# The softmax divisors of an attention: from four small products, a copy and four transposes to one product with repeated ones

## The chip, the cores and the metric

The kernel runs on one core of a Trainium2 chip. A core has engines that each run their own list of instructions in order: TensorE (PE; its weight loads are a row of their own, PEld), VectorE (DVE), ScalarE (ACT), GpSimd (POOL) and SyncE (SP, which issues most of the transfers). TensorE writes its products into eight banks of a small memory (PSUM); VectorE and ScalarE read them from there. The metric is the device time of one execution in microseconds (us).

## What is computed

Two layers of a backbone over 1024 latent tokens with 256 context tokens. Each layer projects the tokens, runs two groups of heads, joins their outputs by one product, and ends in an MLP. One group is an attention with 8 heads of 64 value channels, the other a recurrence (RWKV-7) over the tokens in both directions. The change touches the attention:

```python
def attend(q, k, v):
    s = jnp.einsum('bqhd,bkhd->bhqk', q, k).astype(jnp.float32) * MLA_SCALE
    p = jax.nn.softmax(s, axis=-1).astype(v.dtype)
    return jnp.einsum('bhqk,bkhd->bqhd', p, v)
```

Latent queries see all 1280 keys, context queries the 256 context keys. The kernel forms the exponentials first, multiplies them with the values, and divides at the end by the sum of the exponentials of each query. The change is in how this divisor gets to where it is needed.

## The kernel before, in words

Before and after the two head groups the layers are projections, norms and an MLP, whose products run on TensorE in three passes each (high and low halves). Between them lies one stage per layer, built by `heads`: attention and recurrence together, in one list of work. The profile has these stages at about 510 to 1130 us (layer 0) and 2590 to 3185 us (layer 1).

The attention goes through the heads, and in each head through tiles of queries: two tiles of 512 latent queries, and in layer 0 one of 256 context queries. So there are 16 + 16 tiles of 512 and 8 of 256, 40 in all. In a tile:

- SP loads the queries (`Qraw`), ACT and POOL split them (`Qh`, `Ql`).
- For the maximum of each row, TensorE makes a rough product of queries and keys (L723) and VectorE reduces it (L725, L726), one 128 rows by up to 512 keys at a time.
- For every 128 keys TensorE makes the scores (L750, keys in rows, queries in columns), ACT takes the exponential (`P`, L755), POOL adds it into the kept sums `Ps` (L759), and every second one TensorE multiplies with the values (L744) into `ps_o`, as two halves in rows 0 to 63 and 64 to 127.
- ACT copies one half out (`oa`, L767), VectorE adds the other (`ob`, L768). Now `ob` has 64 channels in rows and the queries in columns.
- The kept sums `Ps` still have 128 rows. `total` (L772) adds them up: per 128 queries a product with `Ps` as weights and one column of ones going past, so that the sums come to lie in rows, one column per 128 queries. VectorE takes the reciprocal of these 4 (or 2) columns (`rc`, L775), POOL repeats each number 64 times along its row (`rx`, L776), TensorE transposes that (`turned`, L780), and VectorE multiplies `ob` by the result (L783). Then `ob` goes to memory by a transfer.

The recurrence goes through 10 steps of 128 tokens in each direction. In a step VectorE masks the products of the tokens (`A`, L391), solves triangular systems by 31 pairs of small instructions that each wait for the one before (`mult` and `total`, L444 and L448), and adds to the states (`S`, L550, L551) and outputs (`ys`, `yo`, L570, L634); TensorE has many small products in between (L387, L401, L411, L481, L493, L527 to L560, L610).

All work in a stage is a list of units. Each has an engine, a duration that its author has written beside it (in ns), what it reads and writes, and for a product that lands in PSUM a kind of bank: six banks `g` serve all of both groups, one bank `o` the values. `Units.run` plays the list through with these durations. At each step it takes, among the units that could start within `slack` ns of the earliest, the one with the longest remaining path, plus a number from `RANKS_HEADS` for its name. The order in which units are taken is the order of the instructions on each engine, for good. It also gives each product a bank: the one of its kind that comes free first by the durations written. On the chip an engine then goes through its instructions in that order, and waits by semaphores where an operand is late or a bank still being read.

Of the kernel before, what the change touches and what calls it, by code (L numbers as in the profile page):

```python
# [12 lines left out]
ALU = mybir.AluOpType  # L13
# [86 lines left out]
def sp_ns(n, k=1):  # L100
# [3 lines left out]


RANKS_IN = {"scaled": 14500, "kf": 1500, "squares k": 4000, "spread c": 19500}
RANKS_HEADS = ({"halves": 6003, "total": -414, "A": 21222, "m1p": -12501, "m1": -28360, "y": -24249, "f2": 3549, "values": -12745, "BKt": -21292,
                "end3": -17483, "yp": -1704, "begin1": -12967, "put": -46488, "f1a": -16985, "f3a": -17647, "f1": -1812, "rows": 2463,
                "sums": -3935, "max": 16985, "mult": -21876, "scores": 798},
               {"begin1": -12967, "f2": -5416, "rows": -1699, "sums": 2772, "max": 16985, "put": -49846, "f3a": -11034, "mult": -34975,  # L110
                "f1a": -36576, "total": 5499, "f1": -2926, "A": 16339, "BKt": -29802, "values": -13309, "y": -24249, "m1": -19796, "yp": -2244,
                "m1p": -12501, "end3": -17483, "scores": 6271, "halves": 19842})
RANKS_OUT = {"copied": -19500, "squares": 28500, "vectors": 14000, "scaled": -7500, "low": -1500, "weights": -7500, "product": -10000, "stage": -3500}


# [150 lines left out]
class Trunk:  # L266
# [36 lines left out]
    def heads(self, li, ard, bvd, pc, gated, ysd, kd, vd, qd, qrd, krr, catd):  # L303

        with ExitStack() as es:
            e1 = self.pool(es, "hd", 1)
            ps = self.pool(es, "hps", 1, space=PSUM)
            banks = {k: [ps.tile([128, 512], F32, name=f"ps_{k}{j}") for j in range(n)] for k, n in (("g", 6), ("o", 1))}
            tiles = {"Y": [ps.tile([128, 32, 16], F32, name=f"ps_Y{li}")]}


            for name, n, shape in (("YF", 1, [128, 32, 32]), ("AX", 1, [128, 32, 32]), ("XM", 1, [128, 32, 32]), ("Y0", 1, [128, 32, 16]), ("tmp", 1, [128, 144]),
# [4 lines left out]
                                   ("Ql", 3, [97, 512]), ("identr", 1, [128, 128]), ("Kh", 2, [97, NT]), ("Kl", 2, [97, NT]), ("Qraw", 1, [96, 512]), ("Kraw", 1, [96, NT])):  # L317
                tiles[name] = [e1.tile(shape, F32R if name in ("Kh", "Kl", "Qh", "Ql", "nm", "identr") else F32, name=f"{name}{li}{j}") for j in range(n)]
            us = Units(59, RANKS_HEADS[li], dict(PE=110, ACT=20, DVE=115, Pool=80, SP=2300), False, True, 0.745, 0.395, 80)
            self.recurrence(us, tiles, li, ard, bvd, pc, gated, ysd, catd)  # L320
            us.group = 1
            self.attention(us, tiles, li, kd, vd, qd, qrd, krr, catd)
            with self.tc.manual_schedule(engines=ENGINES):
                us.run(banks)
# [337 lines left out]
    def attention(self, us, tiles, li, kd, vd, qd, qrd, krr, catd):  # L662


        nc = self.nc
        last = li == L - 1
        qtt = LAT if last else LAT + ALL[:1]
        Kh, Kl, V, Qraw, Qh, Ql, P, Ps, o2, nm, nm3 = (tiles[k] for k in ("Kh", "Kl", "V", "Qraw", "Qh", "Ql", "P", "Ps", "ob", "nm", "nm3"))
        Kraw, o1, rx, rc, identr = (tiles[k][0] for k in ("Kraw", "oa", "rx", "rc", "identr"))
        NK, NQ, NP, NO = len(Kh), len(Qh), len(P), len(o2)  # L670
        c1 = self.c("unit")[:, 1:2]

# [10 lines left out]
        for j in range(NK):  # L683
            us("ACT", act_ns(NT), [], lambda j=j: nc.scalar.copy(Kh[j][64:96], Kraw[64:96]), r=[("Kraw", "rope")], w=[("Kh", j, "rope")])
            us("Pool", pool_ns(NT), [], lambda j=j: nc.gpsimd.tensor_tensor(Kl[j][64:96], Kraw[64:96], Kh[j][64:96].bitcast(F32), op=ALU.subtract),
               r=[("Kraw", "rope"), ("Kh", j, "rope")], w=[("Kl", j, "rope")])
# [18 lines left out]
        def tile(h, p, q, kh, kl, khk, klk, v, vk, e, t0, tl):  # L705
            t, nq = slice(t0, t0 + tl), tl // 128
            nkt = 10 if t0 >= TC else 2
            jr, jq = us.turn("Qraw", len(Qraw)), us.turn("Q", NQ)
            raw, qh, ql, m1, m3 = Qraw[jr], Qh[jq], Ql[jq], nm[jq], nm3[jq]
# [11 lines left out]
            for i in range(nq):  # L721
                for n, (k0, kn) in enumerate(ktt):
                    x = us("PE:max", 140 + kn * 0.28, [], lambda b, i=i, k0=k0, kn=kn: nc.tensor.matmul(b[:, :kn], qh[0:96, 128 * i:128 * i + 128], kh[0:96, k0:k0 + kn], start=True, stop=True), 220,  # L723
                           bank="g", r=[("Qh", jq)] + khk, rows=91)
                    us("DVE", 63 + kn * 1.048, [], lambda b, i=i, n=n, kn=kn: nc.vector.tensor_reduce(m3[:, i, n:n + 1], b[:, :kn], AXIS_X, ALU.max), w=[("nm3", jq, i, n)], free=x)  # L725
            us("DVE", 72, [], lambda: nc.vector.tensor_reduce(m1[:, :nq], m3[:, :nq, :len(ktt)], AXIS_X, ALU.max, negate=True),  # L726
               r=[("nm3", jq, i, n) for i in range(nq) for n in range(len(ktt))], w=[("nm", jq)])
# [5 lines left out]
            x = us("PE:rows", 55 + 111 * nq, [], rows, 200, bank="g", r=[("nm", jq), "identr"], rows=64)  # L733
# [3 lines left out]
            js = us.turn("Ps", 2)  # L737
            sums = Ps[js][:, :tl]
# [8 lines left out]
            for n in range(nkt):  # L747
# [6 lines left out]
                x = us("PE:scores", 60 + tl * 1.344, [], pe, 155, bank="g", r=khk + klk + [("Qh", jq), ("Qh", jq, "row"), ("Ql", jq), ("Ql", jq, "row")], rows=90)  # L754
# [5 lines left out]
                if n % 2:  # L760
                    kw = dict(use=out) if out else dict(bank="o")
                    x = us("PE:values", 84 + 1.805 * tl, [], pair(n - 1, [P[i][:, :tl] for i in jp[-2:]]), r=[("P", i) for i in jp[-2:]] + [vk, ("O", h, t0)], w=[("O", h, t0)], rows=119, **kw)
                    out = out or x

            jo = us.turn("ob", NO)
            o = o2[jo][:, :tl]
            x1 = us("ACT", 180 + tl * 0.835, [], lambda b: nc.scalar.copy(o1[:, :tl], b[64:128, :tl]), r=[("O", h, t0)], w=["oa"], use=out)  # L767
            us("DVE:halves", 75 + tl * 1.04, [], lambda b: nc.vector.tensor_tensor(o, b[0:64, :tl], o1[:, :tl], op=ALU.add), r=["oa", ("O", h, t0)], w=[("ob", jo)], free=out)  # L768

            def total(b):  # L770
                for i in range(nq):
                    nc.tensor.matmul(b[:, i:i + 1], Ps[js][:, 128 * i:128 * i + 128], c1, start=True, stop=True)  # L772

            x = us("PE", 845 / 4 * nq, [], total, 145, bank="g", r=[("Ps", js, 128 * i) for i in range(nq)], rows=1)
            us("DVE", 92, [], lambda b: nc.vector.reciprocal(rc[:, :nq], b[:, :nq]), w=["rc"], free=x)  # L775
            us("Pool", 206 + 54 * nq, [], lambda: nc.gpsimd.tensor_copy(rx[:, :nq], rc[:, :nq].unsqueeze(2).to_broadcast([128, nq, 64])), r=["rc"], w=["rx"])  # L776

            def turned(b):
                for i in range(nq):
                    nc.tensor.transpose(b[0:64, 128 * i:128 * i + 128], rx[:, i], self.ident)  # L780

            x = us("PE", 96 * nq, [], turned, 280, bank="g", r=["rx"], rows=121)
            us("DVE", 75 + tl * 1.04, [], lambda b: nc.vector.tensor_tensor(o, o, b[0:64, :tl], op=ALU.mult), w=[("ob", jo)], free=x)  # L783
            if h < 7:
                us("SP", sp_ns(tl / 2), [], lambda: nc.sync.dma_start(catd[0][q, p, t], o), r=[("ob", jo)])
            else:
# [953 lines left out]
```

## Time and profile before

| | before |
|---|---|
| median of 3 runs | 3976.65 us (3976.02 to 3977.47) |
| profiled execution: its time | 3976.51 us |
| profiled execution: span of the trace | 3974.7 us |
| PE busy | 3819.7 us (96%) |
| DVE busy | 2463.1 us (62%) |
| ACT busy | 1826.9 us (46%) |
| POOL busy | 1267.8 us (32%) |
| mean granted TensorE clock | 0.969 of full speed |

The profile is of one execution. Its instructions carry the line of the kernel and the names of the tiles; a fp32 product shows as two matmuls. Busy times are sums over an engine's own row. An instruction's record holds its start-up too, so records of one engine overlap by some 60 to 90 ns; what an instruction costs its engine in a full queue is read from its start to the start of the next.

### The profile page before, as it was taken

How to read it: one execution, taken by the hardware profiler on the slowest of the kernel's cores; microseconds unless marked ns; L12 is line 12 of the kernel's file. 1: busy time of each engine (PE TensorE's matmuls, PEld its weight loads, DVE VectorE, ACT ScalarE, POOL GpSimd, SP SyncE). 2: the span in 40 equal slices, each digit the busy share in tenths (PEclk: the TensorE clock that was granted, in tenths of full speed). 3: DMA queues.
4: the chain of work that ended last, by engine and by line, in shares of the span. 5: the costliest groups of instructions: out<-in, count | busy, mean ns of one | idle time of the engine just before them, and what ended most of it. 6: DMA issues, size and time to landing. Idle time of an engine off the chain costs nothing.

```text
span 3974.7 us, 66881 instructions
## 1 busy us (share of the span) xinstructions
PE 3819.7 (96%) x26144; PEld 2939.4 (74%) x26144; DVE 2463.1 (62%) x4563; ACT 1826.9 (46%) x3125; POOL 1267.8 (32%) x1850
## 2 busy tenths in 40 slices
PE   5999989999999999999998999999999999999998
PEld 2766766777778888888887766666777688777787
DVE  4476377777537455555337377577778465767666
ACT  4355467777635112222114355567777644333332
POOL 1244174455621000000001244365445704334320
PEclk9999989999999999999999999989899999999999
DMA  6256633332252122222113144532232351111111
GB/s 217 67 172 200 202 117 95 99 102 85 70 171 85 59 80 86 79 70 80 38 43 132 44 153 155 199 112 64 87 106 76 98 189 32 54 43 48 54 48 59
DMA packets 279708, 394.22 MB, mean 99 GB/s; under 512 B 60512, under 2 KB 192576, under 8 KB 279392
## 3 DMA queue, kind: packets, MB, share of 16 engines
q1 hardware_dynamic: 278992, 389.36, 30.7%
q8 instruction: 206, 3.38, 0.4%
q14 instruction: 110, 0.90, 0.1%
q10 hardware_dynamic: 400, 0.59, 0.1%
HBM read 288.45 MB, written 101.42 MB: 98 GB/s over the span
## 4 chain that ended last, share of the span: by engine, by line
PE 76%; DVE 9%; DMA 3%; issue 2%; ACT 2%; POOL 1%; SPq 0%; DVEq 0%; POOLq 0%; ACTq 0%
PE qm L938 41%; PE pm_m L938 8%; PE ps_g L750 5%; PE ps_o L744 3%; PE ps_g L723 2%; PE ps_g L387 2%; PE qm L951 1%; PE ps_g L536 1%; PE ps_g L527 1%; PE ps_g L546 1%; PE ps_g L481 1%; PE ps_g L401 1%; PE ps_g L557 1%; PE ps_g L560 1%; PE pm_n L1192 1%
## 5 line engine op out<-in xcount | busy, mean ns | idle before, releaser
L938 PE MATMUL qm<-hh,wh 128*128 128x512 f32 (+1 forms) x1488 | 556.3, 374 | 6.9 <-DVE x L1536 6.9
L938 PE MATMUL qm<-hh,wl 128*128 128x512 f32 (+1 forms) x1488 | 554.7, 373 | 0.7 <-DVE wl L976 0.7
L938 PE MATMUL qm<-hl,wh 128*128 128x512 f32 (+1 forms) x1488 | 555.0, 373 | 0.0
L759 POOL TENSOR_TENSOR Ps<-Ps,P 128x128 f32<-128x128 f32 x1024 | 433.8, 462 | 308.2 <-ACT P L755 307.9
L975 ACT CAST wh<-wr 128x1024 fp32r<-128x1024 f32 x149 | 155.8, 1045 | 445.6 <-PE qm L938 399.9
L938 PE MATMUL pm_m<-hh,wh 128*128 128x512 f32 (+4 forms) x896 | 339.1, 378 | 3.7 <-ACT o L1251 3.1
L938 PE MATMUL pm_m<-hl,wh 128*128 128x512 f32 (+4 forms) x896 | 330.0, 368 | 1.3 <-POOL hl L925 1.3
L938 PE MATMUL pm_m<-hh,wl 128*128 128x512 f32 (+4 forms) x896 | 330.3, 369 | 0.2 <-DVE wl L976 0.2
L938 PEld LDWEIGHTS qm<-hh,wh 128*128 128x128 f32 x1488 | 279.6, 188 | 64.7 <-DVE x L1536 9.0
L938 PEld LDWEIGHTS qm<-hh,wl 128*128 128x128 f32 x1488 | 280.2, 188 | 55.0 <-DVE wl L976 1.4
L938 PEld LDWEIGHTS qm<-hl,wh 128*128 128x128 f32 x1488 | 279.6, 188 | 55.2 <-DVE hl L1432 1.2
L1536 DVE SCALAR_TENSOR_TENSOR x<-qm,mods,x 128x512 f32<-128x512 f32 x280 | 196.3, 742 | 174.4 <-PE qm L938 174.1
L938 PE MATMUL qm<-uh,wl 128*128 128x512 f32 (+1 forms) x768 | 274.0, 357 | 2.1 <-DVE wl L976 2.1
L938 PE MATMUL qm<-uh,wh 128*128 128x512 f32 (+1 forms) x768 | 275.1, 358 | 0.0
L938 PE MATMUL qm<-ul,wh 128*128 128x512 f32 (+1 forms) x768 | 273.8, 356 | 0.0
L976 DVE TENSOR_TENSOR wl<-wr,wh 128x1024 fp32r<-128x1024 f32 x149 | 187.7, 1260 | 131.1 <-ACT wh L975 130.9
L1459 DVE SCALAR_TENSOR_TENSOR x<-qm,mods,x 128x512 f32<-128x512 f32 x160 | 119.7, 749 | 196.3 <-PE qm L938 192.8
L725 DVE TENSOR_REDUCE nm<-ps_g 128x1 f32<-128x512 f32 (+1 forms) x400 | 213.4, 583 | 38.1 <-PE ps_g L723 36.9
L938 PEld LDWEIGHTS pm_m<-hh,wh 128*128 128x128 f32 (+2 forms) x896 | 169.4, 189 | 68.4 <-issue 31.2
L755 ACT ACTIVATE P<-ps_g 128x512 f32<-128x512 f32 (+1 forms) x336 | 188.6, 586 | 64.9 <-PE ps_g L750 50.4
L938 PEld LDWEIGHTS pm_m<-hl,wh 128*128 128x128 f32 (+2 forms) x896 | 169.3, 189 | 33.6 <-POOL hl L925 2.2
L938 PEld LDWEIGHTS pm_m<-hh,wl 128*128 128x128 f32 (+2 forms) x896 | 169.6, 189 | 30.7 <-issue 0.7
(358 smaller groups left out, 8591.7 us busy)
## 6 DMA issues: line engine op xcount, KB each, us to landing
wr<-in_w SPq DMA_DIRECT2D x90, 512.0 KB, 3.6
BV<-bv SPq DMA_DIRECT2D x40, 768.0 KB, 4.9
raw<-in_ada_w SPq DMA_DIRECT2D x48, 512.0 KB, 3.9
AR<-ar SPq DMA_DIRECT2D x40, 512.0 KB, 7.3
wr<-in_w_in SPq DMA_DIRECT2D x37, 512.0 KB, 3.8
aw<-in_ada_w SPq DMA_DIRECT2D x32, 512.0 KB, 4.2
bv<-bk SPq DMA_DIRECT2D x32, 512.0 KB, 3.0
ar<-ar SPq DMA_DIRECT2D x32, 512.0 KB, 3.6
```

Source lines behind the costliest of these rows:

```text
L387: nc.tensor.matmul(b[:, 128 * j:128 * j + 128], BK[d][half(e), c, p], AR[d][half(e), 2 * p + c], start=True, stop=True)
L723: x = us("PE:max", 140 + kn * 0.28, [], lambda b, i=i, k0=k0, kn=kn: nc.tensor.matmul(b[:, :kn], qh[0:96, 128 * i:128 * i + 128], kh[0:96, ...
L725: us("DVE", 63 + kn * 1.048, [], lambda b, i=i, n=n, kn=kn: nc.vector.tensor_reduce(m3[:, i, n:n + 1], b[:, :kn], AXIS_X, ALU.max), w=[("n ...
L744: nc.tensor.matmul(b[64 * r:64 * r + 64, :tl], v[:, n + r, q], ps[r], start=n == 0, stop=n + 2 == nkt)
L750: nc.tensor.matmul(b[:, :tl], x[:, 128 * n:128 * n + 128], y[:, :tl], start=i == 0, stop=i == 2)
L755: us("ACT", 195 + tl * 0.835, [], lambda b, j=j: nc.scalar.activation(P[j][:, :tl], b[:, :tl], AF.Exp, scale=SCALE), w=[("P", j)], free=x)
L759: us("Pool:sums" if n == 1 else "Pool", 415, [], lambda a=a, b=P[j][:, c:c + 128], c=c: nc.gpsimd.tensor_tensor(sums[:, c:c + 128], a, b, ...
L938: self.nc.tensor.matmul(out, a, b, start=n == 0, stop=n == last)
L975: us("ACT", 947, [], lambda: nc.scalar.copy(wh, raw), r=[key], w=[("wh", j)])
L976: us("DVE:weights", 1135, [], lambda: nc.vector.tensor_tensor(wl, raw, wh.bitcast(F32), op=ALU.subtract), r=[key, ("wh", j)], w=[("wl", j)])
L1459: us("DVE", dve_ns(tl), [u[1]], lambda b: nc.vector.scalar_tensor_tensor(X(m, a), b[:, :tl], self.mods[li][:, 8 * gate + m, s:s + 1], X(m, ...
L1536: z = us("DVE", dve_ns(512), [z], lambda b, m=m, a=a, f=f: nc.vector.scalar_tensor_tensor(X(m, a), b, f, X(m, a), ALU.mult, ALU.add), r=[" ...
```

## The change

One product takes the place of `total` and `turned`: the weights are the column of ones, repeated 64 times, and the kept sums `Ps` go past, 512 (256) columns. Its 64 rows are all the same, the sum of each query's exponentials, in the layout of `ob`. VectorE takes the reciprocal of this whole 64x512 block (into `oa`, which the addition of the halves has by then read) and multiplies `ob` by it. The column `rc`, its repetition `rx` on POOL and the transposes go. The ranks are set anew, the product has a rank of its own name, and `slack`, 59 before, is 67 in layer 0 and 93 in layer 1.

```diff
--- before.py
+++ after.py
@@ -104,12 +104,12 @@
 
 
 RANKS_IN = {"scaled": 14500, "kf": 1500, "squares k": 4000, "spread c": 19500}
-RANKS_HEADS = ({"halves": 6003, "total": -414, "A": 21222, "m1p": -12501, "m1": -28360, "y": -24249, "f2": 3549, "values": -12745, "BKt": -21292,
-                "end3": -17483, "yp": -1704, "begin1": -12967, "put": -46488, "f1a": -16985, "f3a": -17647, "f1": -1812, "rows": 2463,
-                "sums": -3935, "max": 16985, "mult": -21876, "scores": 798},
-               {"begin1": -12967, "f2": -5416, "rows": -1699, "sums": 2772, "max": 16985, "put": -49846, "f3a": -11034, "mult": -34975,
-                "f1a": -36576, "total": 5499, "f1": -2926, "A": 16339, "BKt": -29802, "values": -13309, "y": -24249, "m1": -19796, "yp": -2244,
-                "m1p": -12501, "end3": -17483, "scores": 6271, "halves": 19842})
+RANKS_HEADS = ({"A": 15017, "values": -14650, "BKt": -37124, "y": -8577, "max": 16985, "put": -55711, "m1p": -10723, "sums": 6443,
+                "scores": 10819, "f1": -2328, "total": 1188, "halves": 11193, "f3a": -14590, "end3": 5410, "f2": 3549, "rows": 2774,
+                "begin1": -12967, "m1": -28327, "yp": -349, "mult": -46018, "f1a": -36247, "slack": 67},
+               {"m1": -19227, "yp": -2244, "y": -34405, "mult": -22669, "values": -13309, "BKt": -29802, "rows": 13653, "f1a": -55013, "A": 24283,
+                "f1": -1805, "put": -36636, "f2": 26845, "f3a": -11034, "scores": 6271, "halves": 19842, "m1p": -12501, "end3": -17483,
+                "sums": 1538, "max": 12049, "begin1": -19234, "total": 7372, "slack": 93})
 RANKS_OUT = {"copied": -19500, "squares": 28500, "vectors": 14000, "scaled": -7500, "low": -1500, "weights": -7500, "product": -10000, "stage": -3500}
 
 
@@ -312,11 +312,11 @@
             for name, n, shape in (("YF", 1, [128, 32, 32]), ("AX", 1, [128, 32, 32]), ("XM", 1, [128, 32, 32]), ("Y0", 1, [128, 32, 16]), ("tmp", 1, [128, 144]),
                                    ("Z", 2, [128, 4, 2, 64]), ("BV", 2, [128, 1536]), ("AR", 4, [128, 8, 128]), ("G", 2, [128, 32, 64]), ("XT", 1, [128, 32, 64]),
                                    ("S", 4, [128, 4, 64]), ("ys", 2, [128, 4, 128]), ("gt", 2, [128, 512]), ("sq", 1, [128, 512]), ("rs8", 1, [128, 8]), ("P", 6, [128, 512]),
-                                   ("Ps", 2, [128, 512]), ("oa", 1, [64, 512]), ("ob", 2, [64, 512]), ("rx", 1, [128, 4, 64]), ("rc", 1, [128, 4]), ("nm", 3, [128, 4]),
+                                   ("Ps", 2, [128, 512]), ("oa", 1, [64, 512]), ("ob", 2, [64, 512]), ("nm", 3, [128, 4]),
                                    ("nm3", 3, [128, 4, 3]), ("A", 2, [128, 32, 2, 64]), ("BKt", 1, [128, 32, 64]), ("V", 2, [128, 10, 128]), ("Qh", 3, [97, 512]),
                                    ("Ql", 3, [97, 512]), ("identr", 1, [128, 128]), ("Kh", 2, [97, NT]), ("Kl", 2, [97, NT]), ("Qraw", 1, [96, 512]), ("Kraw", 1, [96, NT])):
                 tiles[name] = [e1.tile(shape, F32R if name in ("Kh", "Kl", "Qh", "Ql", "nm", "identr") else F32, name=f"{name}{li}{j}") for j in range(n)]
-            us = Units(59, RANKS_HEADS[li], dict(PE=110, ACT=20, DVE=115, Pool=80, SP=2300), False, True, 0.745, 0.395, 80)
+            us = Units(RANKS_HEADS[li]["slack"], RANKS_HEADS[li], dict(PE=110, ACT=20, DVE=115, Pool=80, SP=2300), False, True, 0.745, 0.395, 80)
             self.recurrence(us, tiles, li, ard, bvd, pc, gated, ysd, catd)
             us.group = 1
             self.attention(us, tiles, li, kd, vd, qd, qrd, krr, catd)
@@ -666,7 +666,7 @@
         last = li == L - 1
         qtt = LAT if last else LAT + ALL[:1]
         Kh, Kl, V, Qraw, Qh, Ql, P, Ps, o2, nm, nm3 = (tiles[k] for k in ("Kh", "Kl", "V", "Qraw", "Qh", "Ql", "P", "Ps", "ob", "nm", "nm3"))
-        Kraw, o1, rx, rc, identr = (tiles[k][0] for k in ("Kraw", "oa", "rx", "rc", "identr"))
+        Kraw, o1, identr = (tiles[k][0] for k in ("Kraw", "oa", "identr"))
         NK, NQ, NP, NO = len(Kh), len(Qh), len(P), len(o2)
         c1 = self.c("unit")[:, 1:2]
 
@@ -767,20 +767,10 @@
             x1 = us("ACT", 180 + tl * 0.835, [], lambda b: nc.scalar.copy(o1[:, :tl], b[64:128, :tl]), r=[("O", h, t0)], w=["oa"], use=out)
             us("DVE:halves", 75 + tl * 1.04, [], lambda b: nc.vector.tensor_tensor(o, b[0:64, :tl], o1[:, :tl], op=ALU.add), r=["oa", ("O", h, t0)], w=[("ob", jo)], free=out)
 
-            def total(b):
-                for i in range(nq):
-                    nc.tensor.matmul(b[:, i:i + 1], Ps[js][:, 128 * i:128 * i + 128], c1, start=True, stop=True)
-
-            x = us("PE", 845 / 4 * nq, [], total, 145, bank="g", r=[("Ps", js, 128 * i) for i in range(nq)], rows=1)
-            us("DVE", 92, [], lambda b: nc.vector.reciprocal(rc[:, :nq], b[:, :nq]), w=["rc"], free=x)
-            us("Pool", 206 + 54 * nq, [], lambda: nc.gpsimd.tensor_copy(rx[:, :nq], rc[:, :nq].unsqueeze(2).to_broadcast([128, nq, 64])), r=["rc"], w=["rx"])
-
-            def turned(b):
-                for i in range(nq):
-                    nc.tensor.transpose(b[0:64, 128 * i:128 * i + 128], rx[:, i], self.ident)
-
-            x = us("PE", 96 * nq, [], turned, 280, bank="g", r=["rx"], rows=121)
-            us("DVE", 75 + tl * 1.04, [], lambda b: nc.vector.tensor_tensor(o, o, b[0:64, :tl], op=ALU.mult), w=[("ob", jo)], free=x)
+
+            x = us("PE:total", 45 + 1.79 * tl, [], lambda b: nc.tensor.matmul(b[0:64, :tl], c1.to_broadcast([128, 64]), sums, start=True, stop=True), 160, bank="g", r=[("Ps", js, c) for c in range(0, tl, 128)], rows=121)
+            us("DVE", 75 + tl * 1.04, [], lambda b: nc.vector.reciprocal(o1[:, :tl], b[0:64, :tl]), w=["oa"], free=x)
+            us("DVE", 75 + tl * 1.04, [], lambda: nc.vector.tensor_tensor(o, o, o1[:, :tl], op=ALU.mult), r=["oa"], w=[("ob", jo)])
             if h < 7:
                 us("SP", sp_ns(tl / 2), [], lambda: nc.sync.dma_start(catd[0][q, p, t], o), r=[("ob", jo)])
             else:
```

The new ranks and the new lengths move instructions all through both stages. Two places show what matters for the divisors. In the tables below `ps_g_3470` to `ps_g_3475` are the six banks `g` of layer 0, a row is a line of the kernel, an operation, what it writes and reads, its columns, and in brackets what it waits for. In the kernel after, L771 is the new product, L772 the reciprocal of 64x512 and L773 the multiplication; lines up to L768 are the same in both.

On TensorE, at the second tile of layer 0, before: the sums go into bank 3471, the transposes of another tile's divisors into 3470, and bank 3471 is written again after those, a pair of values (L744), a group of scores (L750) and two row maxima (L723).

```order
L772 MATMUL ps_g_3471<-ct,Ps_3511 128x1 [waits Activation_49,Pool_49]
L772 MATMUL ps_g_3471<-ct,Ps_3511 128x1 [waits Pool_49] x3
L780 MATMUL ps_g_3470<-ct,rx_3515 64x128 [waits Activation_49,Pool_49]
L780 MATMUL ps_g_3470<-ct,rx_3515 64x128 x3
L744 MATMUL ps_o_3476<-P_3504,V_3526 64x512
L744 MATMUL ps_o_3476<-P_3505,V_3526 64x512
L750 MATMUL ps_g_3475<-Qh_3528,Kh_3536 128x512 [waits Activation_49]
L750 MATMUL ps_g_3475<-Qh_3528,Kl_3538 128x512
L750 MATMUL ps_g_3475<-Ql_3531,Kh_3536 128x512
L723 MATMUL ps_g_3474<-Kh_3536,Qh_3529 128x512 [waits Activation_49]
L723 MATMUL ps_g_3470<-Kh_3536,Qh_3529 128x512 [waits DVE_49]
L723 MATMUL ps_g_3471<-Kh_3536,Qh_3529 128x512 [waits DVE_49]
```

The same tile after: the sums go into bank 3473, three products for row maxima follow, and then comes one of the recurrence (L493) into bank 3473 again.

```order
L771 MATMUL ps_g_3473<-Ps_3511,ct 64x512 [waits Activation_49,Pool_49]
L723 MATMUL ps_g_3474<-Kh_3534,Qh_3527 128x512 [waits Activation_49]
L723 MATMUL ps_g_3475<-Kh_3534,Qh_3527 128x512
L723 MATMUL ps_g_3470<-Kh_3534,Qh_3527 128x512
L493 MATMUL ps_g_3473<-XT_3493,XM_3480 32x32 [waits DVE_49,Activation_49]
L493 MATMUL ps_g_3473<-XT_3493,XM_3480 32x32 [waits Activation_49]
L493 MATMUL ps_g_3473<-XT_3493,XM_3480 32x32 x14
L723 MATMUL ps_g_3471<-Kh_3534,Qh_3527 128x512
```

So the transposes are gone, and the bank of the sums, which VectorE frees by its reciprocal, is now wanted again after three products.

On VectorE, around the second tile's reciprocal, before: the multiplication of one tile, the reciprocal of 4 columns, and then work of the recurrence (L444, L448), row maxima (L725) and the next tile's halves (L768).

```order
L783 TENSOR_TENSOR ob_3513<-ob_3513,ps_g_3470 64x512 [waits PE_49]
L775 RECIPROCAL rc_3516<-ps_g_3471 128x4 [waits Pool_49]
L444 TENSOR_TENSOR tmp_3482<-AX_3479,ps_Y_3477 128x31 [waits Activation_49]
L725 TENSOR_REDUCE nm_3521<-ps_g_3474 128x1 [waits PE_49]
L768 TENSOR_TENSOR ob_3514<-ps_o_3476,oa_3512 64x512 [waits Activation_49]
L448 TENSOR_TENSOR ps_Y_3477<-ps_Y_3477,tmp_3482 128x31 [waits DVE_49]
L725 TENSOR_REDUCE nm_3521<-ps_g_3470 128x1 [waits PE_49]
L725 TENSOR_REDUCE nm_3521<-ps_g_3471 128x1 [waits PE_49]
```

The same reciprocal after: it has 512 columns, the multiplication (L773) follows one instruction later, and behind these stand the row maxima of four banks.

```order
L772 RECIPROCAL oa_3512<-ps_g_3473 64x512 [waits PE_49]
L444 TENSOR_TENSOR tmp_3482<-AX_3479,ps_Y_3477 128x100 [waits DVE_49]
L773 TENSOR_TENSOR ob_3514<-ob_3514,oa_3512 64x512 [waits DVE_49]
L448 TENSOR_TENSOR ps_Y_3477<-ps_Y_3477,tmp_3482 128x25x4 [waits DVE_49]
L725 TENSOR_REDUCE nm_3519<-ps_g_3474 128x1 [waits PE_49]
L725 TENSOR_REDUCE nm_3519<-ps_g_3475 128x1 [waits PE_49]
L725 TENSOR_REDUCE nm_3519<-ps_g_3470 128x1 [waits PE_49]
L725 TENSOR_REDUCE nm_3519<-ps_g_3471 128x1 [waits PE_49,Activation_49]
```

The multiplication, which stood ahead of or far behind its reciprocal, now follows it at once, and the row maxima stand right behind both.

## Rows read from the trace of the kernel before

**Rows 1.** The page: TensorE's busy time; the chain that ended last, by engine.

```profile
PE 3819.7 (96%) x26144; PEld 2939.4 (74%) x26144; DVE 2463.1 (62%) x4563; ACT 1826.9 (46%) x3125; POOL 1267.8 (32%) x1850
...
PE 76%; DVE 9%; DMA 3%; issue 2%; ACT 2%; POOL 1%; SPq 0%; DVEq 0%; POOLq 0%; ACTq 0%
```

**Rows 2.** Busy times by stretch, both stages: stretch, length, busy time per engine, clock, DMA.

```profile
500.00:1131.00 631.00, 603.22 (x6898) 434.31 (x6899) 440.55 (x1158) 440.00 (x792) 364.88 (x694) 0.94 0.32 94
2565.00:3190.00 625.00, 591.51 (x6518) 429.32 (x6517) 436.46 (x1120) 431.74 (x762) 344.63 (x659) 0.92 0.32 97
```

**Rows 3.** DVE's groups by shape, 512 to 1130: busy us, mean ns | idle before.

```profile
L768 DVE TENSOR_TENSOR ob<-ps_o,oa 64x512 f32<-64x512 f32 x16 | 10.8, 677 | 9.0 <-ACT oa L767 8.7
...
L768 DVE TENSOR_TENSOR ob<-ps_o,oa 64x256 f32<-64x256 f32 x8 | 3.3, 412 | 6.8 <-ACT oa L767 6.8
...
L775 DVE RECIPROCAL rc<-ps_g 128x4 f32<-128x4 f32 x16 | 2.8, 176 | 11.1 <-PE ps_g L772 11.1
L621 DVE TENSOR_SCALAR rs<-ps_g 128x8 f32<-128x8 f32 x10 | 1.7, 166 | 13.8 <-PE ps_g L618 13.7
L775 DVE RECIPROCAL rc<-ps_g 128x2 f32<-128x2 f32 x8 | 1.3, 166 | 5.2 <-ACT P L755 3.7 <-PE ps_g L772 1.4
```

**Rows 4.** DVE in order of time, two reciprocals: start us, length us, instruction.

```profile
1055.62 0.15 DVE L775 RECIPROCAL rc<-ps_g 128x2 f32<-128x2 f32 x1
1055.70 0.66 DVE L634 TENSOR_TENSOR yo<-ps_g,yo 128x512 f32<-128x512 f32 x1
...
3005.48 0.17 DVE L775 RECIPROCAL rc<-ps_g 128x4 f32<-128x4 f32 x1
3005.57 3.05 DVE L725 TENSOR_REDUCE nm<-ps_g 128x1 f32<-128x512 f32 x5
```

**Rows 5.** PE in order of time: sums, transposes, a 128x512 fp32 product.

```profile
893.60 0.95 PE L772 MATMUL ps_g<-ct,Ps 128*128 128x1 f32 x8
894.48 3.37 PE L387 MATMUL ps_g<-AR,BV 64*128 64x128 f32 x40
897.78 0.63 PE L780 MATMUL ps_g<-ct,rx 128*64 128x128 f32 x4
898.16 0.37 PE L750 MATMUL ps_g<-Qh,Kh 97*128 97x256 f32 x1
...
990.61 1.02 PE L610 MATMUL ps_g<-ys,ct 128*128 128x512 f32 x2
991.57 1.08 PE L744 MATMUL ps_o<-P,V 128*64 128x512 f32 x4
```

**Rows 6.** PE in order of time, behind the sums at 3003.96.

```profile
3004.88 1.47 PE L723 MATMUL ps_g<-Kh,Qh 96*128 96x512 f32 x4
3006.28 1.08 PE L744 MATMUL ps_o<-P,V 128*64 128x512 f32 x4
3007.29 0.50 PE L723 MATMUL ps_g<-Kh,Qh 96*128 96x512 f32 x1
3007.63 0.40 PE L750 MATMUL ps_g<-Qh,Kh 97*128 97x512 f32 x1
```

**Rows 7.** DVE in order of time, a reciprocal with idle time around it.

```profile
2804.59 0.18 DVE L775 RECIPROCAL rc<-ps_g 128x4 f32<-128x4 f32 x1 [1.10 <-PE ps_g L772]
2807.41 1.24 DVE L429 STREAM_TRANSPOSE AX<-YF 64x1024 f32<-64x1024 f32 x1 [2.63 <-ACT YF L424]
```

**Rows 8.** Waits, 512 to 1130: who waited for whom, us in total, times, longest.

```profile
POOL rx L776 <- DVE rc L775: 29.9, 10, 8.8
```

**Rows 9.** DVE in order of time, the last two tiles of layer 0.

```profile
1116.56 0.68 DVE L768 TENSOR_TENSOR ob<-ps_o,oa 64x512 f32<-64x512 f32 x1 [6.76 <-ACT oa L767]
...
1123.42 0.41 DVE L783 TENSOR_TENSOR ob<-ob,ps_g 64x256 f32<-64x256 f32 x1 [2.18 <-PE ps_g L780]
```

**Rows 10.** PE in order of time, a product of scores at each clock.

```profile
2639.89 0.63 PE L750 MATMUL ps_g<-Qh,Kl 97*128 97x512 f32 x1
...
3007.86 0.40 PE L750 MATMUL ps_g<-Qh,Kl 97*128 97x512 f32 x1
```

## The prediction

> **What bounds the kernel now.** I read the page first: TensorE is busy for 96% of the span and holds 76% of the chain that ended last [rows 1]. Then the busy times of the two stages that the change touches, 631 and 625 us long: TensorE is busy for 603.22 and 591.51 us of them, VectorE for 440.55 and 436.46, GpSimd for 364.88 and 344.63 [rows 2]. So TensorE bounds both stages, with 28 and 33 us idle, and VectorE has 190 and 189 us, 379 together. But each engine goes through a fixed list, and TensorE gets a bank back only when VectorE or ScalarE has read it: idle time of VectorE is worth something only where nothing that TensorE wants stands behind the long instruction. Last I read the places of the divisors in order of time, on VectorE and on TensorE. Nothing outside the stages changes.
>
> **TensorE's part.** Removed per tile of 512: eight passes of sums, 893.60 to 894.48, 0.88 us, and four transposes, 897.78 to 898.16, 0.38 us [rows 5], together 1.26. Added: one fp32 product past which 512 columns go. The trace has such a product with 128 columns of weights, L610: 990.61 to 991.57, 0.96 us [rows 5]; with 64 columns of weights I take the same, since the 512 that go past are what takes the time. That gives back 0.30 us for each of 32 tiles, 9.6, and I take half as much for each of the 8 tiles of 256, 1.2: 11 us in all, all on the engine that bounds. Bounds: 0, where the sums stood in a gap, and 0.88 + 0.38 - 0.48 per tile, were the new product half as long, 25 us.
>
> **GpSimd, transfers, latency.** The copies `rx` go, and with them waits of GpSimd for the reciprocal (29.9 us in layer 0, ten times [rows 8]). GpSimd has 266 us idle in that stage [rows 2], and the sums `Ps` that it adds wait for exponentials, so this is worth 0. The round trip over GpSimd and TensorE goes too, but it matters only where nothing else is left, at the end of a stage. In layer 0 the last two tiles took from 1116.56 to 1123.42 + 0.41, 7.27 us [rows 9]. Their chain after is two additions, two reciprocals and two multiplications on VectorE alone: with the lengths of [rows 3] and below, 2 x (0.68 + 0.41) + 3.0 + 1.6 = 6.8 us. So the end of the stage comes no later; 0. The transfer of `ob` is issued by the same queue behind the same multiplication; 0.
>
> **VectorE's part: the reciprocal.** Removed: a reciprocal of 4 or 2 numbers per row, which held the engine for 0.08 to 0.09 us from its start to the next one's [rows 4]. The multiplication stays. Added: a reciprocal of 512 (256) numbers per row. The list of work has it at the price of an addition, and an addition of 512 is recorded with 677 ns, one of 256 with 412 [rows 3]: (677 - 412) / 256 = 1.04 ns a number. The reciprocals of the trace speak against that price. With 2 numbers the mean is 166 ns, with 4 it is 176 [rows 3]: 5 ns a number. A multiply-add of 8 numbers takes 166 ns, thus about 158 without its numbers at 1.04 each; against this the 4 numbers of the reciprocal take 18 ns and the 2 take 8, 4 to 4.5 ns each [rows 3]. From start to start it is 0.09 us against 0.08 [rows 4], again 5 ns. So a reciprocal seems to pass a number in some 5 of the times in which an addition passes one, and 512 take 156 + 512 x 5 = 2.7 us. The differences are of 10 ns in records that scatter by as much, so I bound it widely: below by the addition, 0.68 us, above by twice the slope, 156 + 512 x 10 = 5.3 us. I take 3.0 us, near the rows, a little up because the step is read from so few numbers; 1.6 us for 256.
>
> The Trainium skill, "VectorE: DVE Perf Modes", section "First, the fixed hardware budget", says that the reciprocal is an iterative divide with a repeat count of 8. The trace agrees that a reciprocal pays more per number than an addition, though with 5 ns, not eight times 1.04. By eight passes the estimate would be 156 + 512 x 8.3 = 4.4 us a tile, and the sum below some 25 us higher.
>
> **What of it reaches TensorE.** VectorE gets 32 x (3.0 - 0.1) + 8 x (1.6 - 0.1) = 105 us more. What stands behind the reciprocal and waits: the order tables show its own bank first (wanted by TensorE after three row maxima), and the maxima of four more banks. I counted TensorE's work between each new product and the next write to that product's bank, in the new order, with lengths of the trace: a row maximum of 512 keys 0.35 us (3004.88 to 3006.28, four), a pair of values 1.01 (3006.28 to 3007.29) [rows 6], a small product of 128 columns 0.08 (894.48 to 897.78, forty) [rows 5], and so on. For the 32 tiles of 512 it is 0.9 us at the least, 2.1 us in the middle, above 3.2 us in six. The bank is held for 3.0 us and some 0.2 us to get in and out; summing 3.2 less the cover over the tiles gives 33 us of waiting, and next to nothing for the tiles of 256. That is the least at this length, since the reciprocal may start late and the banks of the maxima behind it are wanted as well: in before, after 3004.88, TensorE writes the fifth maximum at 3007.29 and scores from 3007.63 [rows 6], while the five reductions behind that reciprocal run for 3.05 us from 3005.57 [rows 4]; 2.9 us later, they would end at 3011.5, and six banks are full long before. The most is all 105 us. At other places the engine had nothing to do: the reciprocal at 2804.59 came after 1.10 us of idle time and was followed by 2.63 us more [rows 7]; there it costs almost nothing. I take half, 52 us, nearer to the least, because that one is counted.
>
> **The sum.** 3976.5 (the profiled execution; the median of the runs is 3976.65, the same within 0.2) - 11 + 52 = 4017.5: 4018 us. The new ranks and `slack` move everything else as well; they were set for lengths in which the reciprocal is 0.6 us, and I put them at 0, with 10 us to either side.
>
> **The rivals.**
> - *The reciprocal passes numbers as an addition does* (faster). Then it holds its bank for 0.9 us, no cover in my count is shorter, and TensorE keeps its 11 us and up to 10 from the new order: 3955 to 3966, say 3964. For it: four numbers are little to read a slope from. Against it: three comparisons give 4 to 5 ns. It decides below about 2 us for 512, where the waits counted as above (11 us at 2.2 us of holding) are as large as what TensorE saves. Chance 0.17.
> - *VectorE's idle time hides it.* With 379 us of it [rows 2] only a fifth of the 105 us may reach TensorE: 21 - 11 = +10, 3987. Against it: the bank's count alone gives 33. Chance 0.12, and half of it within 0.2%.
> - *VectorE becomes the bound.* All of it reaches TensorE, since the recurrence's small instructions wait behind it too: 3976.5 + 105 - 11 = 4070. For it: the reciprocal cannot be split, and whatever stands behind it is late by its whole length. Against it: in layer 0 VectorE would be busy for 440 + 58 of 631 us, far from full. Chance 0.13.
> - *The clock follows.* In the stages it is granted at 0.94 and 0.92 [rows 2], and a product of scores that takes 0.40 us at 2.4 GHz takes 0.63 at 1.2 GHz [rows 10]. The slow stretches lie where TensorE had gaps or small products; 52 us of new gaps could bring as many slow ones again. At 60 us more of slow clock, half of it lost: +30, 4048. Chance 0.10.
>
> The forecast itself has 0.48. A measurement of this kernel can tell 0.2%, 8 us, from no change. Faster by more than that: 0.18, the first rival and a little of the new order; within: 0.07; slower: 0.75. The range for 8 in 10 goes from 3957 to 4085: below it lies part of the first rival, above it a reciprocal of 4.4 us or more of which most reaches TensorE. The forecast's own range is 3990 to 4060.
>
> **What would show it.** The group of the reciprocal at 64x512: about 3.0 us each says that the slope was read rightly, 0.7 that the first rival holds. TensorE's waits for VectorE at the line after the new product, in both stages some 50 us more of idle time. The new product at 0.96 us from start to start. VectorE's busy time about 100 us up. The stage of layer 0 and that of layer 1 both about 20 us longer, and nothing outside them. I am wrong if the reciprocal is long and the stages are not, or if TensorE's waits come from elsewhere.

## The result, and the profile after

The changed kernel takes 4029.96 us (median of 4 runs, 4027.23 to 4035.06), the kernel before 3977.06 beside it: a ratio of 1.0138, 95% interval [1.0119, 1.0158], by which it is 55 us slower. The forecast was 4018 in a range of 3957 to 4085. The profiled execution took 4029.63 us, its span 4027.9.

The page, TensorE's busy time and the chain that ended last, as [rows 1]:

```profile
PE 3837.7 (95%) x25792; PEld 2919.5 (72%) x25792; DVE 2559.1 (64%) x4563; ACT 1827.3 (45%) x3125; POOL 1256.5 (31%) x1810
...
PE 72%; DVE 14%; DMA 2%; issue 2%; ACT 2%; POOL 1%; SPq 0%; ACTq 0%; DVEq 0%; POOLq 0%
```

VectorE's part of the chain rose from 9% to 14%, its busy time by 96 us. The two stages, cut with the same margins and columns as [rows 2]:

```profile
501.60:1167.80 666.20, 617.17 (x6702) 429.16 (x6703) 498.04 (x1159) 440.14 (x794) 358.88 (x670) 0.90 0.30 90
2601.10:3243.10 642.00, 590.05 (x6360) 410.25 (x6359) 475.27 (x1120) 432.78 (x762) 339.65 (x643) 0.92 0.31 95
```

They are 35.2 and 17.0 us longer, 52.2 of the 53.2 us by which the span grew, so what the change does happens in them. TensorE's idle time is the length less its busy time: 61 us before, 101 after. The granted clock fell in layer 0 from 0.94 to 0.90. With two levels, 1.2 and 2.4 GHz, a mean of c says that 2 x (1 - c) of the length lay at the lower one: 76 + 100 = 176 us before, 133 + 103 = 236 after (two decimals leave some 6 us open in each stage; the trace's unrounded records of the clock give 181 and 234). Only what of it falls on busy time costs anything: by the same records 163 us before, 210 after. Half of the 47 us more is work done late, 24. So 52 us longer are 40 of gaps, 24 of the clock, and about 11 less of work.

VectorE's groups by shape, over the whole span, columns as in [rows 3]:

```profile
L772 DVE RECIPROCAL oa<-ps_g 64x512 f32<-64x512 f32 x32 | 107.0, 3342 | 17.0 <-PE ps_g L771 16.9
L773 DVE TENSOR_TENSOR ob<-ob,oa 64x512 f32<-64x512 f32 x32 | 26.4, 824 | 0.3
...
L772 DVE RECIPROCAL oa<-ps_g 64x256 f32<-64x256 f32 x8 | 14.0, 1750 | 11.0 <-PE ps_g L771 10.9
```

The reciprocal takes 3.34 us, five times the addition of 512 (0.677 us [rows 3]) at whose price the list has it; (3342 - 1750) / 256 is 6.2 ns a number. Who waited for it (engine, tile and line: us, times):

```profile
  PE ps_g L723: 8.1, 4
...
  PE ps_g L387: 5.9, 5
...
  PE ps_g L411: 3.8, 4
  PE ps_g L731: 3.6, 2
```

With three smaller groups TensorE's waits put down to it are 28.0 us. One of them, in order of time on TensorE (start, length, instruction, idle time ahead and its end):

```profile
2677.43 1.07 PE L771 MATMUL ps_g<-Ps,ct 128*64 128x512 f32 x2
2678.43 1.43 PE L723 MATMUL ps_g<-Kh,Qh 96*128 96x512 f32 x5
2682.28 0.58 PE L723 MATMUL ps_g<-Kh,Qh 96*128 96x256 f32 x1 [2.42 <-DVE oa L772]
2682.80 1.98 PE L744 MATMUL ps_o<-P,V 128*64 128x512 f32 x4
```

The new product takes 1.00 us from start to start. Five products for row maxima follow, as many as there are other banks `g`. The next one waits until the reciprocal ends: it needs the bank of the sums, and VectorE is still reading it:

```profile
2678.89 3.34 DVE L772 RECIPROCAL oa<-ps_g 64x512 f32<-64x512 f32 x1
2682.16 0.22 DVE L444 TENSOR_TENSOR tmp<-AX,ps_Y 128x130 f32<-128x130 f32 x1
2682.30 0.67 DVE L773 TENSOR_TENSOR ob<-ob,oa 64x512 f32<-64x512 f32 x1
```

The gap is paid twice. Behind it four products of values take 1.98 us, where the same four took 1.08 [rows 6]; in tens of us around it (columns as for the stages) the clock goes from 1.00 to 0.66 and back:

```profile
2670.00:2680.00 10.00, 9.86 (x41) 5.57 (x39) 9.65 (x30) 4.75 (x8) 10.00 (x23) 1.00 0.08 21
2680.00:2690.00 10.00, 7.72 (x20) 3.50 (x21) 8.91 (x21) 1.04 (x2) 2.19 (x6) 0.66 0.06 14
2690.00:2700.00 10.00, 9.71 (x44) 5.49 (x42) 6.85 (x19) 9.44 (x15) 10.00 (x21) 1.00 0.00 0
```

### The profile page after: what moved, and what is told of

Same layout as the page of the kernel before. It is cut to its first block, busy times and chain, and to the rows that moved or that the text cites. A ratio compares the mean times of both kernels' runs of the same rounds, so it can differ in the third digit from the quotient of the medians.

```text
span 4027.9 us, 66072 instructions
## 1 busy us (share of the span) xinstructions
PE 3837.7 (95%) x25792; PEld 2919.5 (72%) x25792; DVE 2559.1 (64%) x4563; ACT 1827.3 (45%) x3125; POOL 1256.5 (31%) x1810
## 4 chain that ended last, share of the span: by engine, by line
PE 72%; DVE 14%; DMA 2%; issue 2%; ACT 2%; POOL 1%; SPq 0%; ACTq 0%; DVEq 0%; POOLq 0%
PE qm L928 41%; PE pm_m L928 8%; PE ps_g L750 4%; PE ps_o L744 3%; DVE oa L772 2%; PE ps_g L387 2%; PE qm L941 2%; PE ps_g L723 1%; DVE ps_Y L448 1%; DVE nm L725 1%; DVE tmp L444 1%; PE ps_g L536 1%; PE pm_n L1182 1%; PE ps_g L527 1%; PE ps_g L557 1%
## 5 line engine op out<-in xcount | busy, mean ns | idle before, releaser
L725 DVE TENSOR_REDUCE nm<-ps_g 128x1 f32<-128x512 f32 (+1 forms) x400 | 216.0, 582 | 48.2 <-PE ps_g L723 46.8
```

## The experiments

Kernels ran in several sessions, in which the kernel before had medians of 3971 to 3980, so differences are taken between ratios: 0.001 is 4.0 us.

**1. The reciprocal's length alone** (order kept).

```
-nc.vector.reciprocal(o1[:, :tl], b[0:64, :tl])
+nc.vector.tensor_copy(o1[:, :tl], b[0:64, :tl])
```

> The changed kernel with its order kept, but VectorE copies the sums where it took the reciprocal (64x512 at about 0.4 to 0.7 us in place of 3.34); so it multiplies by the sums instead of dividing. Theory A (the reciprocal's length makes the loss, through banks and work behind it on VectorE): the loss goes and TensorE's saving is left, 3950 to 3972 us. Rival B (the new order of both stages makes the loss, whatever the reciprocal takes): 4010 us or more. In between, 3985 to 4005, would say that each makes about half.

3936.28 us, ratio 0.9908 [0.9877, 0.9939]: 37 us faster than before, 91 faster than the changed kernel. That is below theory A's range: the reciprocal's length costs more than either theory had. Its copy and its stages:

```profile
L772 DVE COPY oa<-ps_g 64x512 f32<-64x512 f32 x32 | 21.6, 676 | 16.9 <-PE ps_g L771 16.8
```

```profile
500.50:1115.90 615.40, 587.88 (x6702) 410.67 (x6703) 451.99 (x1159) 439.93 (x793) 363.10 (x670) 0.95 0.33 97
2549.30:3149.30 600.00, 569.13 (x6358) 400.14 (x6357) 436.63 (x1120) 433.05 (x763) 345.78 (x643) 0.94 0.34 102
```

TensorE has the same instructions in the same order as in the changed kernel, so the two can be compared instruction by instruction. The stages are 92.8 us shorter: 42.6 of idle time, and 50.2 of busy time. About 40 of the 50 are the clock: the products that ran at the lower clock only in the changed kernel take 51 us longer there, those that did so only here 11 us less. Nearly all of the other 10 is in products that ran at the higher clock in both, more than half of it in the first product behind a gap. So the slow clock cost about as much as the gaps that led to it.

With each wait put down to what ended it, the changed kernel's 42.6 us more of idle time are 28 for the reciprocal itself, 10 for VectorE's other results (9 of them the recurrence's, 1 the row maxima), 8 for ScalarE's, and 4 less for transfers.

**2. The ranks alone**: the changed kernel with the ranks and `slack` of before (the table goes back too).

```
-us = Units(RANKS_HEADS[li]["slack"], RANKS_HEADS[li], ...
+us = Units(59, RANKS_HEADS[li], ...
```

> The changed kernel with the ranks and the slack of 59 of the kernel before, the new product without a rank. Theory A: the reciprocal costs its 3.34 us wherever the order puts it, 4010 to 4050 us, within some 15 us of the changed kernel. Rival B: with the old ranks the loss goes, 3985 us or less.

4081.23 us, 1.0271 [1.0236, 1.0307]; a miss: without the new ranks the change would lose 108 us, not 55.

**3. The true price in the list**, ranks kept.

```
-us("DVE", 75 + tl * 1.04, [], lambda b: nc.vector.reciprocal(...
+us("DVE", 65 + tl * 6.22, [], lambda b: nc.vector.reciprocal(...
```

> The changed kernel with one number changed: the list has the reciprocal at 65 + 6.22 ns per number, as the chip takes it, so that the order is made for 3.25 us instead of 0.61. Theory A: the list then asks for the bank and for the work behind it later, and TensorE's waits for the reciprocal (some 25 us) mostly go: 3985 to 4012 us; VectorE's busy time stays. Rival B: no better than the changed kernel, 4020 to 4040, or worse, since the ranks were made for the other length.

4032.57 us, 1.0149 [1.0115, 1.0183]: theory A misses, its rival holds. A price set right under ranks that were set with the wrong one brings nothing.

**4. The dose doubled**: the same reciprocal taken twice.

```
-lambda b: nc.vector.reciprocal(o1[:, :tl], b[0:64, :tl])
+lambda b: [nc.vector.reciprocal(o1[:, :tl], b[0:64, :tl]) for _ in range(2)]
```

> The changed kernel with its order kept and every reciprocal done twice in a row (the same result): VectorE gets another 32 x 3.34 + 8 x 1.75 = 121 us. Theory A: the cover between the product and the next use of its bank is used up by the first, so that most of the second reaches TensorE: +85 to +125 us over the changed kernel, 4115 to 4155. Rival C (VectorE's idle time takes it up, and what the change costs is gaps that drop the clock, not length): +30 to +60, 4060 to 4090.

4198.91 us, 1.0576 [1.0534, 1.0618]: 174 us more for 121 us more of VectorE's work, above the range. Its stages:

```profile
500.50:1258.80 758.30, 648.14 (x6702) 450.88 (x6703) 566.31 (x1183) 440.72 (x793) 355.79 (x670) 0.84 0.26 79
2695.00:3412.70 717.70, 619.76 (x6362) 430.22 (x6361) 527.26 (x1136) 434.19 (x762) 339.68 (x643) 0.85 0.28 85
```

Against the first experiment: 150 us more of idle time and 111 more of busy time with the same products, so again mostly the clock.

**5. The new ranks under the old divisors.**

```
-us = Units(59, RANKS_HEADS[li], ...
+us = Units(RANKS_HEADS[li]["slack"], RANKS_HEADS[li], ...
```

> The kernel before with the ranks and slacks of the changed one (67 and 93), everything else as before. So far: the new work with a copy in place of the reciprocal ran at 3936, 35 us under before; with the reciprocal and the old ranks at 4081, 51 over the changed kernel. Theory A2 (the new ranks shorten the stages by themselves): 3935 to 3965 here. Rival B2 (the ranks fit the new work alone, and the 35 us come from the new product): 3970 or more.

3975.56 us, 1.0001 [0.9982, 1.0021]. The theory that the new order is better in itself falls.

**6. The bank set free early**: ScalarE copies the sums out of it.

```
+us("ACT", 180 + tl * 0.835, [], lambda b: nc.scalar.copy(o1[:, :tl], b[0:64, :tl]), w=["oa"], free=x)
+us("DVE", 75 + tl * 1.04, [], lambda: nc.vector.reciprocal(o1[:, :tl], o1[:, :tl]), w=["oa"])
```

> The changed kernel, but ScalarE copies the sums out of the bank (0.58 us) and VectorE takes the reciprocal from there, at the same length. The bank of the sums comes free early; what stands behind the reciprocal on VectorE waits as before. Theory D (the reciprocal's own bank is what TensorE waits for): 3975 to 4000. Rival E (the row maxima and the recurrence's work behind it on VectorE): 4010 to 4040.

4083.36 us, 1.026 [1.0229, 1.0292]: neither theory. One unit more reordered the whole stage, so the time doesn't tell whether the bank that is held or VectorE's queue behind it costs more. The trace shows what came in place of the waits for the bank. TensorE waits 0.2 us for the copy that frees it, but 38.6 us in 24 waits for row maxima, against 4.9 us in 11 in the changed kernel; most of it here (us, times, longest):

```profile
PE ps_g L723 <- DVE nm L725: 21.3, 13, 3.6
```

It shows too that the bank isn't why the reciprocal is long; from the sums' copy it takes the same:

```profile
L773 DVE RECIPROCAL oa<-oa 64x512 f32<-64x512 f32 x32 | 106.7, 3334 | 7.2 <-ACT oa L772 7.2
```

**7. Copies under the old ranks**: the edits of the first and the second experiment together.

```
-nc.vector.reciprocal(o1[:, :tl], b[0:64, :tl])
+nc.vector.tensor_copy(o1[:, :tl], b[0:64, :tl])
...
+us = Units(59, RANKS_HEADS[li], ...
```

> The changed kernel with the old ranks and slack 59, and with a copy in place of the reciprocal, so that it multiplies by the sums instead of dividing. Against the run with the reciprocal and the old ranks (4081) it gives the price of the reciprocal in the old order; against before (3971 to 3977) what the new product, without GpSimd's copy and the transposes, is worth with no new ranks. Theory A2: the ranks give most of the 35 us, so 3960 to 3980 here. Rival B2: the new product gives them, 3935 to 3950.

3984.36 us, 1.0013 [0.9994, 1.0032]: 4 us above the range of theory A2, the nearer one, though its interval reaches into it. The new product alone, at the price that the list has, brings nothing in the old order. Its stages, and TensorE's waits for row maxima (us, times, longest), which were 1.2 us in five waits before:

```profile
502.00:1131.50 629.50, 591.16 (x6702) 410.69 (x6703) 456.96 (x1159) 442.32 (x793) 360.96 (x670) 0.95 0.32 95
2564.60:3187.50 622.90, 579.78 (x6362) 400.09 (x6361) 448.18 (x1120) 432.18 (x762) 343.00 (x643) 0.93 0.32 98
```

```profile
PE ps_g L723 <- DVE nm L725: 14.1, 17, 3.5
```

The busy time fell by 24 us, of which 16 are the clock (163 us of busy time at the lower level before, 130 here), but the idle time rose by 20. The four kernels of experiments 1, 2, 7 and the change make a square: the reciprocal costs 103 us in the old order and 91 in the new, the new ranks bring 42 with copies and 53 with reciprocals. The two add up almost freely: 103 and 91 differ by no more than their intervals.

**8. Half the numbers per row.** The sums of the two halves of a tile go to rows 0 to 63 and 64 to 127, and one reciprocal of 128x256 does both; priced truly.

```
+nc.tensor.matmul(b[64 * r:64 * r + 64, :hl], c1.to_broadcast([128, 64]), sums[:, hl * r:hl * r + hl], ...
...
+us("DVE", 65 + 6.22 * hl, [], lambda b: nc.vector.reciprocal(rr, b[:, :hl]), w=["rc"], free=x)
```

> A version that keeps the new product but spreads the reciprocal over all 128 rows: the sums of the first half of a tile's queries come to rows 0 to 63, those of the second half to rows 64 to 127 (two products of 256 columns side by side), the halves of the values are added into the same layout by two additions of 256 columns, and one reciprocal of 128x256 and one multiplication of 128x256 follow; two transfers put the tile away. Priced in the list as the chip takes it. VectorE per tile of 512: 0.41 x 2 + 1.75 + 0.41 = 3.0 us against 4.7 in the changed kernel and 2.0 with a copy. Theory A (length of the reciprocal): between the copy's 3936 and the changed kernel's 4030, near the copy since 1.75 us is within the cover of most tiles: 3940 to 3970, so better than before. Rival B (the order): 4000 or more.

4002.95 us, 1.0059 [1.0035, 1.0083]: theory A misses, and rival B's 4000 or more holds, though it is 31 us better than the changed kernel. 128 rows cost what 64 do:

```profile
L780 DVE RECIPROCAL rc<-ps_g 128x256 f32<-128x256 f32 x32 | 56.0, 1750 | 14.8 <-PE ps_g L777 11.5 <-ACT XM L485 3.1
```

**9 to 11. Orders searched anew** in a replay of the list's own rule: for the split (9), for the changed kernel with the true price (10), and as a control for the kernel before (11). Against experiment 8, experiment 3 and the kernel before only the table differs, with its `slack`; cut, the tenth's:

```
-RANKS_HEADS = ({"A": 15017, "values": -14650, "BKt": -37124, ...
+RANKS_HEADS = ({'A': 4656, 'values': -12846, 'BKt': -9040, ...
```

> The kernel of e8_split, with ranks and slack of the heads stages searched anew for its own units and prices (a replay of the list's rule, in which the lists end about 45 us earlier over both layers than with the ranks it had). Theory A (what the change loses is the reciprocal's 3.34 us at a place that others wait for, and an order that doesn't fit: with the short reciprocal and an order set for it the new divisors win): 3925 to 3965 us, under the kernel before. Rival B (the list's clock has little to do with the chip's, and ranks searched on it bring nothing): 3985 to 4020 us, as e8_split or worse.

> The changed kernel with the reciprocal priced at what it takes (65 ns and 6.22 ns a number) and the ranks searched anew at that price; all instructions are those of the changed kernel, only their order differs. Theory A (about 14 us of the added waits go with an order that knows the price; the long reciprocal stays before the products of values): 3985 to 4025 us, still slower than before. Rival C (the whole loss was a stale order): 3955 to 3975 us.

> The control: the kernel before, with ranks searched in the same way (nothing was found for the first layer, whose order is unchanged; in the second the list ends 10 us earlier). If a search alone is worth little: 3960 to 3985 us. If searched ranks bring as much to the old divisors as to the new ones: below 3950 us.

3983.98 us, 1.0028 [1.0000, 1.0055]; 4008.44, 1.0078 [1.0051, 1.0106]; 3983.09, 1.0020 [0.9999, 1.0041]. The tenth came out as expected: an order that knows the price takes back 24 of the 55 us. The split ends between its two theories and doesn't pass the kernel before: 45 us that the list reckoned were 12 on the chip, less than the intervals can tell from none. The control shows the same: 10 us gained by the list's reckoning were none on the chip.

**12. A dose in between** (order kept): half of the columns divided, half copied.

```
+nc.vector.reciprocal(o1[:, :tl // 2], b[0:64, :tl // 2])
+nc.vector.tensor_copy(o1[:, tl // 2:tl], b[0:64, tl // 2:tl])
```

> The changed kernel, with the reciprocal taken of half of the columns of a unit and a copy of the other half, so that the step takes about 1.75 + 0.37 = 2.1 us where it took 3.34 us with the reciprocal of all and 0.68 us with copies alone; order and ranks kept. (It multiplies half of the outputs by their sums instead of dividing.) Theory A (each step's length counts in proportion, 94 us for 40 steps that are 2.6 us longer): 3936 + 94 x 1.45/2.66 = about 3987 us, 3975 to 4000. Rival B (a threshold: VectorE's gaps take up a step of 2 us, and only what is longer is paid): 3930 to 3955 us. Rival C (any step longer than what the list reckons is paid in full): above 4005 us.

3979.44 us, 0.9996 [0.9973, 1.0019]: in theory A's range, at its lower end. With experiments 1 and 4 and the changed kernel there are four doses in one order. VectorE's time at the step, and where it lay above the one before:

| the step, 512 columns | VectorE in all | ratio | us per us more of VectorE | TensorE's waits for the step |
|---|---|---|---|---|
| copy, 0.68 us | 25 us | 0.9908 | | 0 |
| half, 2.1 us | 76 us | 0.9996 | 0.7 | 7.4 us |
| reciprocal, 3.34 us | 121 us | 1.0138 | 1.3 | 28.0 us |
| twice, 6.7 us | 242 us | 1.0576 | 1.4 | 103.4 us |

The intervals leave 0.3 open in the first two slopes and 0.15 in the third, so the last two can't be told apart. There is no threshold, then, but a slope that is steeper above 2 us than below. There the kernel loses more than VectorE's added time, and the traces of experiments 1 and 4 show why: a gap on TensorE is followed by products at the lower clock. 2.1 us is also where the change breaks even.

## Why the prediction was right, and where it was not

The direction, the size and the mechanism came out: the reciprocal is long, and TensorE waits for it. That the sum came within 12 us is luck: two terms were wrong by about 40 us, with opposite signs, and nearly cancelled; a third was off by 16.

- *The reciprocal's length*: 3.0 us forecast, 3.34 measured; 1.6 and 1.75 for 256. The slope of 5 ns that was read from rows of 2 and 4 numbers [rows 3] is 6.2. The addition of VectorE's busy time, about 100 us, was 96. The Trainium skill, "VectorE: DVE Perf Modes", "First, the fixed hardware budget", gives the iterative divide a repeat count of 8. By this trace a number costs six times an addition's 1.04 ns, and the estimate of 4.4 us that the prediction worked out from the page was 1.1 us too long; the measurement decides.
- *TensorE's saving*: the product at 1.00 us, forecast 0.96, gives back 0.26 x 32 + 1 = 9 us instead of 11, on the engine's own count; 8 of the 24 us of busy time in experiment 7 agree. But that run has +5 us where -11 was forecast: its order gave the saving back in 20 us more of waiting, 13 of them for row maxima at L723. That TensorE's idle time elsewhere stays as it is was an unspoken step, and it failed.
- *What of the reciprocal reaches TensorE*: half of 105 us, 52, was forecast; experiment 1 against the changed kernel gives 91, experiment 7 against 2 gives 103. The step that failed is "nearer to the least, because that one is counted". The count, 33 us, was of gaps alone, and the gaps were near it: 43 us more of idle time in experiment 1. Of the 50 us more of busy time that it lacks, some 40 are the clock's, which stood among the rivals (4048, chance 0.10) and should have been a term of the sum: wherever gaps were forecast, the slow stretch behind them belonged to them.
- *The new ranks*, put at 0 with 10 us to either side: they bring 42 to 53 us with the new work, and nothing with the old (experiment 5). This term hid the error of the one before: -11 + 52 + 0 = 41 forecast, +5 + 91 - 42 = 54 measured. That they "move everything else as well" was no reason for 0. They were set for this work with a short reciprocal, and a good part of their worth stays when it is long.
- *The first rival* (the reciprocal as an addition, 3964): the reciprocal is not that short; and were it, the kernel would be at 0.9908, some 3940. Its point of decision, "below about 2 us", was right, but by luck: it set 11 us of waits against 11 us saved, where the half dose costs 35 us over the copy (0.0088) and the copy stands 37 under the kernel before.
- *Idle time hides it* (3987) and *VectorE becomes the bound* (4070) fall by the traces: 0.7 to 1.4 us are lost for each us added, and VectorE is busy for 498 of 666 us. In size the second came close (91 of 96 us reach TensorE), but by gaps and the clock in about equal parts, not by a full VectorE.
- *The stages*: about 20 us each was forecast, 35 and 17 measured, nothing outside. Layer 0 has nearly all of the time at the lower clock that was added, 49 of 53 us by the unrounded records.
- *Waits of about 50 us at the line after the new product*: 28.0 are put down to it, of 40 more in all. Against experiment 1, which has the same order, waits for the reciprocal itself grew by 28 us and those for VectorE's work behind it by 10, so in this order the held bank costs more than the queue. No run shows that freeing the bank helps: in experiment 6, in another order, waits for row maxima took the place of those for the bank. Still open is whether some order lets the split divisors win; none that ran was faster than the kernel before with the divisions done.

## What to carry to other kernels

An operation that moves work off the engine that bounds is paid where the other engine does it: read its duration per number from the smallest rows there are, and hold it against the work that covers its bank, not against the other engine's idle time. A new gap on TensorE costs its length, and where the clock falls behind it more: here 40 us of clock for 43 of gaps. An order set by ranks is part of the change: old ranks under the new work would have cost as much again as the whole result (53 us), and an order searched at the true price took back nearly half of it (24).

## What was not expected of the hardware

A reciprocal takes 6.2 ns for each number in a row, whether 64 or 128 rows (1750 ns for 64x256 and for 128x256) and whether it reads a bank or SBUF (3342 and 3334 ns for 64x512). And a delay off the engine that bounds cost more than its own length: the second reciprocal, 121 us of VectorE's time, made the kernel 174 us slower. Where the reciprocal took the place of the copy, about 40 of the 93 us by which the stages grew were the same products at a lower clock.
